# The product for u in one float32 pass, and a shorter read-back of the chunk kernel

## The chip, the cores and the metric

The kernel runs on one core of a Trainium2 chip. The metric is the device time of one execution in microseconds (us), the median of three runs. The engines of a core work in parallel, each through its own queue and in order: PE (TensorE: matrix products and transposes, results in PSUM), DVE (VectorE), ACT (ScalarE), POOL (GpSimd) and SP, which here only issues DMAs. ACT and POOL issue DMAs as well. All DMAs share 16 DMA engines.

## The reference, cut to what matters

One decoder layer on 256 tokens of width 2048, in float32:

```python
h = rmsnorm(x, ln1_g)
q, k, v, u = split(h @ w_in)                  # 1024, 256, 256, 1024 columns
a = sliding_window_attention(q, k, v)         # QK-norm, bias, sinks
y = gelu(S5(u) + d * u)                       # 64 groups of 16 channels, 64 complex states each
s = y * sigmoid(y @ w_glu)
x = x + concat(rmsnorm(a), rmsnorm(s)) @ w_out
x = x + (silu(h2 @ w_gate) * (h2 @ w_up)) @ w_down      # h2 = rmsnorm(x)
```

S5 is a linear recurrence over time with a complex diagonal, one input matrix b and one output matrix c for each group.

## The kernel before

**Large products.** Each large product takes weights in pieces of 256 rows by 512 columns (512 KB), which SP loads into four buffers (`raw`, tag "w"). A piece is split into two parts of a shorter float type, fp32r: `whi`, a copy by ACT (line 455), and `wlo`, the rest by DVE (line 456), two buffers of each. The left operand is split likewise (`hT`, `lT` for x). `block` (lines 490 to 506) adds three products for each of the two 128-token halves: hi x hi, hi x lo and lo x hi, each with 512 columns. A piece so has 12 matmuls. There are 16 pieces for u, 24 for q, k and v, 8 for the GLU, 32 for the output projection and 264 for the SwiGLU.

**x.** Four tiles `xt[0..3]` of 512 KB hold x transposed. They lie in memory that is used later for other things: `sm[0]`, `sm[1]`, `qn[0]`, `qn[1]`. `split_x` writes hT (ACT, 16 instructions) and lT (DVE, 16) with the norm's gain; ACT then squares xt in place for the token sums, from which r1, the norm's factor, comes. The result of the u blocks is scaled by r1 into `qn`, and goes through DRAM (`ud`) to turn it from tokens into chunks.

**The S5 part** works in chunks of T = 8 tokens, in four quarters q of 16 groups, with these steps for each quarter: `matrices` in two halves (m0a, m0b, ...: six DVE operations of 1024 columns each, small PE products and transposes), `tokens` (u0: reads u from DRAM as chunks, transposes it on PE), `rotations` (r0: the angles), `states` (s0: PE products, a scan on DVE), `outputs` (o0: 32 PE products with the chunk's kernel `m` and with the carried state, written to DRAM as `zd`). The string STEPS gives the order in which they are put to the scheduler. `issue_after(marks[n])` holds instructions behind piece n of the weights on the same engine: U_AT for the copy in `tokens` (ACT), PY_AT for `outputs` (PE), GELU_AT for the GELU (ACT). Pieces 0 to 15 are those of u, 16 to 39 those of q, k and v. The blocks of q, k and v run beside the S5 steps; the GLU needs all four quarters.

**The chunk's kernel.** Output t of a chunk takes input s <= t with tap t - s, so `m` is a Toeplitz matrix, [8 inputs x 16 channels, 8 outputs x 16 groups x 16 channels]. `matrices` writes the 8 taps to DRAM (`kd`, four DMAs of 32 KB), behind 7 taps of zeros that were written at the start, and one DMA of 1 MB reads them back with a step of one tap for each input, zeros included. All these DMAs are issued by POOL:

```python
m = self.sp.tile([P, T, GC, GP], F32, name="mt", tag="mt", bufs=2)
nc.gpsimd.dma_start(m.rearrange("p t g q -> p (t g q)"),
                    dap(kd, [[GC * GP, T], [TAPS * GC * GP, GP], [1, T * GC * GP]]))
```

POOL also issues the loads of u's chunks (`ut`), of the S5 result (`sm` from `zd`), and computes the small powers.

Of the kernel before, what the change touches and what calls it, by code (L numbers as in the profile page):

```python
# [2 lines left out]

# [1 line left out]

# [5 lines left out]
F32 = mybir.dt.float32  # L11
# [7 lines left out]
P = 128  # L19
# [20 lines left out]
WORK = dict(tag="t", bufs=4)  # L40


STEPS = "m0a m0b u0 u1 r0 m1a s0 m1b u2 r1 o0 s1 m2a u3 r2 m2b r3 o1 s2 m3a m3b o2 s3 o3"

U_AT = (11, 12, 19, 20)
PY_AT = (21, 27, 34, 39)
GELU_AT = (38, 39, 39, 39)

HEADS = [0, 4, 1, 5, 2, 6, 3, 7, 8, 12, 9, 13, 10, 14, 11, 15]

# [3 lines left out]
C2 = float(np.float32(round((TWO_PI - C1) * 2.0**20) / 2.0**20))  # L54
C3 = float(np.float32(TWO_PI - C1 - C2))
MAGIC = 12582912.0
TAPS = 2 * T - 1
UB = 4 * GP


# [4 lines left out]
def bc(ap, pos, n):  # L65
    dims = [list(d) for d in ap.ap]
    dims.insert(pos, [0, n])
    return bass.AP(ap.tensor, ap.offset, dims)
# [10 lines left out]
class Ssm:  # L79
# [8 lines left out]
    def load(self):  # L88
        self.a = self.sp.tile([P, 2 * G], F32, name="sa")
        self.ldt = self.sp.tile([G, 3], F32, name="ldt")  # L90
        self.nc.sync.dma_start(self.ldt[:, 0:1], self.ins["ssm_log_dt"].rearrange("(g o) -> g o", o=1))
        self.nc.sync.dma_start(self.a, self.ins["ssm_a"])
        self.kts = [self.sp.tile([P, T, 4, GP], F32, name=f"kt{i}") for i in range(2)]
        self.kd = [self.dpool.tile([GP, TAPS, GC * GP], F32, name=f"kd{q}") for q in range(G // GC)]
        zero = self.sp.tile([GP, GC * GP], F32, name="zero")
        self.nc.gpsimd.memset(zero, 0.0)
        for kd in self.kd:
            self.nc.gpsimd.dma_start(kd[:, : T - 1], bc(zero, 1, T - 1))
        self.bc = []
        self.cm, self.bm, self.m, self.u, self.h, self.rot = ([[] for _ in range(G // GC)] for _ in range(6))  # L100
        self.sign = self.sp.tile([P, 1], F32, name="sign")
        self.nc.vector.memset(self.sign, 1.0)
        self.nc.vector.memset(self.sign[NS:], -1.0)
# [127 lines left out]
    def matrices(self, q, h):  # L231

        nc, v, s = self.nc, self.nc.vector, self.nc.scalar
        b, c = self.bc[q]
        ft, lam = self.ft, self.lam
        HG = GC // 2
        hs = slice(h * HG, (h + 1) * HG)
        gh = slice(q * GC + h * HG, q * GC + (h + 1) * HG)
        cmh = self.sp.tile([P, HG, T + 1, GP], F32, name="cm", tag="cm", bufs=4)
        s.activation(cmh[:, :, 0], c[:, 0, hs], AF.Copy, scale=self.sign[:, 0:1])  # L240
        tm = self.sp.tile([P, HG, T, GP], F32, name="tm", tag="tm")
        for dst, i in ((cmh[:, :, 1:], 0), (tm, 1)):
            e = lam[:, i, 1 : T + 1, gh].rearrange("p t g -> p g t")
            v.tensor_tensor(dst, bc(c[:, i, hs], 2, T), bc(e, 3, GP), op=ALU.mult)
        v.tensor_tensor(cmh[:, :, 1:], cmh[:, :, 1:], tm, op=ALU.subtract)
        bmh = self.sp.tile([P, HG, P], F32, name="bm", tag="bm", bufs=4)
        bm2 = self.sp.tile([P, HG, T, GP], F32, name="bm2", tag="bm2", bufs=2)
        tm2 = self.sp.tile([P, HG, T, GP], F32, name="tm2", tag="tm")
        for dst, i in ((bm2, 0), (tm2, 1)):
            e = ft[:, i, :, gh].rearrange("p t g -> p g t")  # L250
            v.tensor_tensor(dst, bc(b[:, i, hs], 2, T), bc(e, 3, GP), op=ALU.mult)
        v.tensor_tensor(bm2, bm2, tm2, op=ALU.add)
        pk = self.ps.tile([P, 2, T, GP], F32, name="pk", **WORK)
        for i in range(HG):
            gq, g4 = divmod(i, 4)
            nc.tensor.matmul(pk[32 * g4 : 32 * g4 + 32, gq].rearrange("p t q -> p (t q)"),
                             lhsT=bm2[:, i, 0:2].rearrange("p t q -> p (t q)"),
                             rhs=cmh[:, i, :T].rearrange("p t q -> p (t q)"), start=True, stop=True)
        kt = self.kts[q % 2]
        kv = kt[:, :, 2 * h : 2 * h + 2]  # L260
        s.copy(kv.rearrange("p t g q -> p g t q"), pk)
        v.tensor_tensor(kv[:, 0], kv[:, 0], self.dg[:, 4 * q + 2 * h : 4 * q + 2 * h + 2], op=ALU.add)
        for n in range(HG // 4):
            pt = self.ps.tile([P, 4, P], F32, name="pt_bm", **WORK)
            for i in range(4):
                nc.tensor.transpose(pt[:, i], bm2[:, 4 * n + i].rearrange("p t q -> p (t q)"), self.cst["ident"])  # L266
            s.copy(bmh[:, 4 * n : 4 * n + 4], pt)
        self.cm[q] += [cmh[:, i, 1:].rearrange("p t q -> p (t q)") for i in range(HG)]
        self.bm[q] += [bmh[:, i] for i in range(HG)]
        if h == 0:  # L270
            return
        kd = self.kd[q]
        for g4 in range(4):
            nc.gpsimd.dma_start(kd[:, T - 1 :, 4 * GP * g4 : 4 * GP * (g4 + 1)],
                                kt[32 * g4 : 32 * g4 + GP].rearrange("p t g q -> p t (g q)"))
        m = self.sp.tile([P, T, GC, GP], F32, name="mt", tag="mt", bufs=2)
        nc.gpsimd.dma_start(m.rearrange("p t g q -> p (t g q)"),
                            dap(kd, [[GC * GP, T], [TAPS * GC * GP, GP], [1, T * GC * GP]]))
        self.m[q] = [m[:, :, 4 * (g % 4) + g // 4] for g in range(GC)]

    def tokens(self, q, behind):

        nc, s = self.nc, self.nc.scalar
        ut = self.sp.tile([P, T, 4 * GP], F32, name="ut", tag="ut")
        nc.gpsimd.dma_start(ut.rearrange("p t x -> p (t x)"),
                            dap(self.ud, [[T * UB, P], [1, T * UB]], 4 * q * L * UB))
        pu = self.ps.tile([P, 4, P], F32, name="pu", **WORK)
        uq = self.sp.tile([P, 4, T, GP], F32, name="uq", tag="uq")
        last = ut[:, T - 1]
        with self.tc.issue_after(behind):  # L290
            s.copy(uq, bass.AP(last.tensor, last.offset, [list(last.ap[0]), [GP, 4], [-UB, T], [1, GP]]))
        for gq in range(4):
            nc.tensor.transpose(pu[:, gq], uq[:, gq].rearrange("p t q -> p (t q)"), self.cst["ident"])
        u = self.sp.tile([P, GC, NCH], F32, name="ua", tag="ua", bufs=4)
        s.copy(u.rearrange("p (a b) c -> p b a c", b=4), pu.rearrange("p b (a c) -> p b a c", c=NCH))
        self.u[q] = u
# [131 lines left out]
class Weights:  # L428
# [8 lines left out]
    def fetch(self, src):  # L437
        w = self.raw.tile([P, KD, NB], F32, name="w", tag="w")
        self.nc.sync.dma_start(w, src)
        self.ready.append(w)  # L440

    def piece(self, src):
        was, self.tc.cur_priority = self.tc.cur_priority, self.place
        out = self._piece(src)
        self.place, self.tc.cur_priority = self.tc.cur_priority, was
        return out
# [14 lines left out]
def layer_kernel(ctx: ExitStack, tc: tile.TileContext, ins, out):  # L461
# [28 lines left out]
    def block(hi, lo, wsrc, k0=0):  # L490
# [14 lines left out]
            wts.marks[-1].append(mm.ins)  # L505
        return acc

    def pieces(w, nb, kg0, kgs):
        return [w[nb, kg] for kg in range(kg0, kg0 + kgs)]

# [51 lines left out]
        ssm.coefficients(0, nc.sync)  # L562
    with prio(-99_990):
        ssm.coefficients(1, nc.sync)
    def split_x(k4):
        for i in range(4):
            k = 4 * k4 + i
            s.activation(hT[:, k], xt[k4][:, i], AF.Copy, scale=g1[:, k : k + 1])
            v.scalar_tensor_tensor(lT[:, k], xt[k4][:, i], g1[:, k : k + 1], hT[:, k].bitcast(F32),
                                   op0=ALU.mult, op1=ALU.subtract)  # L570

    with prio(9_000):
        for k4 in range(4):
            split_x(k4)
    with prio(9_500):
        ssm.tables()
    with prio(9_400):
        for k4 in range(4):
            s.activation(xt[k4], xt[k4], AF.Square)
        ssx = token_sums([xt[k // 4][:, k % 4] for k in range(16)], "ssx", sp, "an")  # L580
        r1 = rsqrt_mean(ssx, D, NT, "r1")


# [13 lines left out]


    ngc = G // GC
    with prio(26_500):  # L600
        for q in range(2, ngc):
            ssm.coefficients(q, nc.sync, sm[q - 2])
    for nb in range(SW // NB):
        with prio(30_000 + 2_000 * nb):
            acc = block(hT, lT, pieces(ins["w_u"], nb, 0, 16 // KD))
            for t in range(NT):
                un = qn[t][:, nb * NB : (nb + 1) * NB]
                s.activation(un, acc[t], AF.Copy, scale=r1[:, t : t + 1])
                nc.scalar.dma_start(ssm.ud[nb * (NB // UB) : (nb + 1) * (NB // UB), t * P : (t + 1) * P]
                                    .rearrange("b p x -> p b x"), un.rearrange("p (b x) -> p b x", x=UB))  # L610
    with prio(60_000):
        for nb in (2, 0, 1):
            acc = block(hT, lT, pieces(ins["w_qkv"], nb, 0, 16 // KD))
# [6 lines left out]
    with prio(20_000):  # L620
        for step in STEPS.split():
# [1 line left out]
            if step[0] == "m":  # L623
                ssm.matrices(q, "ab".index(step[2]))
            elif step[0] == "u":
                ssm.tokens(q, marks[U_AT[q]][0])
            elif step[0] == "r":
                ssm.rot[q] = ssm.rotations(q)
            elif step[0] == "s":
# [275 lines left out]
```

## Time and profile before

| | us |
|---|---|
| median of three runs | 1096.76 (1092.87 to 1099.7) |
| profiled execution, its own time | 1101.14 |
| its span | 1099.3 |
| PE busy in it | 1048.4 (95%) |
| DVE busy | 622.4 (57%) |
| ACT busy | 502.7 (46%) |
| from the start to the first product of the GLU | 201.9 |

The first 204 us hold u, q, k, v and the S5 part; then come the GLU and the attention with the output projection as filler (to about 350 us), and the SwiGLU to the end. From 250 us on PE is busy in nearly every slice.

### The profile page before, as it was taken

To read this page: it belongs to the slowest core of one execution; us is meant where nothing else is said; L and a number is where in the kernel's file an instruction comes from. 1 tells how busy PE (TensorE), PEld (TensorE's weight loads), DVE (VectorE), ACT (ScalarE), POOL (GpSimd) and SP (SyncE) were. 2 spreads that over 40 slices of the span, in tenths; PEclk is the share of its full clock that TensorE was granted. 3 is DMA by queue.
4 is the path that set the end of the run, shared out by engine and by line. 5 is a ranking of instruction groups with operands and counts; after the bars stand their busy time and mean duration, and the time that the engine had idled before them with its cause. 6 is when DMAs were issued, how large, how long until landed. Compare 5 with 4: busy or idle time off the path is not lost.

```text
span 1099.3 us, 13352 instructions
## 1 busy us (share of the span) xinstructions
PE 1048.4 (95%) x5120; PEld 833.5 (76%) x5120; DVE 622.4 (57%) x761; ACT 502.7 (46%) x689; POOL 42.3 (4%) x62
## 2 busy tenths in 40 slices
PE   6999794799999999999999999999999999999998
PEld 4776573577788888888888888888888888888886
DVE  6998685488756544554445544554445444444443
ACT  7454354376546544444444444444444333333332
POOL 1011012500000000000000000000000000000000
PEclk9999898899999999999999999999999999999999
DMA  8766565462455555555555555555555556565653
GB/s 323 222 192 162 131 171 164 146 206 97 135 173 191 168 179 190 190 192 181 187 189 191 191 181 185 191 190 188 186 186 189 190 187 202 189 207 191 209 182 107
DMA packets 62127, 201.45 MB, mean 183 GB/s; under 512 B 11440, under 2 KB 13792, under 8 KB 61296
## 3 DMA queue, kind: packets, MB, share of 16 engines
q1 hardware_dynamic: 52656, 184.83, 51.5%
q0 software_dynamic: 3520, 11.58, 4.1%
q10 hardware_dynamic: 5888, 4.20, 1.3%
q8 instruction: 40, 0.66, 0.3%
q14 instruction: 23, 0.19, 0.1%
HBM read 195.38 MB, written 5.20 MB: 182 GB/s over the span
## 4 chain that ended last, share of the span: by engine, by line
PE 83%; DMA 6%; DVE 6%; ACT 3%; issue 2%; POOL 0%; SPq 0%; ACTq 0%; DVEq 0%; POOLq 0%
PE acc L502 26%; PE acc L503 26%; PE acc L501 26%; DMA w<-in_w_qkv 3%; DVE wlo L456 2%; DMA zd<-za 2%; PE pt_f L833 1%; DMA mt<-kd 1%; ACT whi L455 1%; PE po L745 1%; DMA sa<-in_ssm_a 1%; PE pl L707 0%; PE pp L739 0%; PE pt_bm L266 0%; PE pq L517 0%
## 5 line engine op out<-in xcount | busy, mean ns | idle before, releaser
L456 DVE TENSOR_TENSOR wlo<-w,whi 128x1024 fp32r<-128x1024 f32 x344 | 421.1, 1225 | 411.1 <-ACT whi L455 410.8
L455 ACT CAST whi<-w 128x1024 fp32r<-128x1024 f32 x344 | 362.1, 1053 | 495.5 <-PE acc L503 474.3
L502 PE MATMUL acc<-wlo,pTh 128*128 128x512 f32 x704 | 276.3, 392 | 0.1
L503 PE MATMUL acc<-whi,pTl 128*128 128x512 f32 x704 | 276.0, 392 | 0.1
L501 PE MATMUL acc<-whi,pTh 128*128 128x512 f32 x704 | 274.5, 390 | 0.0
L503 PEld LDWEIGHTS acc<-whi,pTl 128*128 128x128 f32 x704 | 133.3, 190 | 26.6 <-DVE pTl L537 0.5
L501 PEld LDWEIGHTS acc<-whi,pTh 128*128 128x128 f32 x704 | 132.2, 188 | 27.6 <-ACT pTh L536 0.5
L502 PEld LDWEIGHTS acc<-wlo,pTh 128*128 128x128 f32 x704 | 132.2, 188 | 27.4 <-DVE wlo L456 0.5
L502 PE MATMUL acc<-wlo,fhi 128*128 128x512 f32 x352 | 140.5, 399 | 0.0
L501 PE MATMUL acc<-whi,fhi 128*128 128x512 f32 x352 | 138.7, 394 | 0.0
L503 PE MATMUL acc<-whi,flo 128*128 128x512 f32 x352 | 138.1, 392 | 0.0
L502 PE MATMUL acc<-wlo,hT 128*128 128x512 f32 x160 | 65.9, 412 | 13.9 <-DVE wlo L456 13.8
L501 PEld LDWEIGHTS acc<-whi,fhi 128*128 128x128 f32 x352 | 66.1, 188 | 17.2
L503 PEld LDWEIGHTS acc<-whi,flo 128*128 128x128 f32 x352 | 66.1, 188 | 15.6
L502 PEld LDWEIGHTS acc<-wlo,fhi 128*128 128x128 f32 x352 | 66.1, 188 | 15.2
L501 PE MATMUL acc<-whi,hT 128*128 128x512 f32 x160 | 62.8, 407 | 12.0 <-ACT whi L455 12.0
L503 PE MATMUL acc<-whi,lT 128*128 128x512 f32 x160 | 65.3, 408 | 0.0
L501 PE MATMUL acc<-whi,mT 128*128 128x512 f32 x128 | 50.9, 398 | 0.8 <-ACT mT L536 0.8
L502 PE MATMUL acc<-wlo,mT 128*128 128x512 f32 x128 | 50.5, 394 | 0.0
L503 PE MATMUL acc<-whi,nT 128*128 128x512 f32 x128 | 50.3, 394 | 0.0
L502 PEld LDWEIGHTS acc<-wlo,hT 128*128 128x128 f32 x160 | 30.9, 193 | 24.7 <-DVE wlo L456 17.7
L501 PEld LDWEIGHTS acc<-whi,hT 128*128 128x128 f32 x160 | 30.8, 194 | 20.2 <-ACT whi L455 13.2
(251 smaller groups left out, 771.0 us busy)
## 6 DMA issues: line engine op xcount, KB each, us to landing
w<-in_w_gu SPq DMA_DIRECT2D x176, 512.0 KB, 3.5
w<-in_w_down SPq DMA_DIRECT2D x88, 512.0 KB, 4.3
w<-in_w_out SPq DMA_DIRECT2D x32, 512.0 KB, 3.5
w<-in_w_qkv SPq DMA_DIRECT2D x24, 512.0 KB, 3.8
w<-in_w_u SPq DMA_DIRECT2D x16, 512.0 KB, 4.5
mt<-kd POOLq DMA_DIRECT2D x4, 1024.0 KB, 15.4
w<-in_w_glu SPq DMA_DIRECT2D x8, 512.0 KB, 4.9
bias<-td POOLq DMA_DIRECT2D x4, 512.0 KB, 4.5
```

The source lines that it names most:

```text
L455: self.marks.append([nc.scalar.copy(hi, w).ins])
L456: nc.vector.tensor_tensor(lo, w, hi.bitcast(F32), op=ALU.subtract)
L501: mm = pe.matmul(acc[t], lhsT=xh, rhs=whi, start=first, stop=False)
L502: pe.matmul(acc[t], lhsT=xh, rhs=wlo, start=False, stop=False)
L503: pe.matmul(acc[t], lhsT=xl, rhs=whi, start=False, stop=last)
L745: pe.matmul(po[a * HD : (a + 1) * HD, :, t], lhsT=kvn[kb][:, kv * HD : (kv + 1) * HD], rhs=pT[:, b, a], start=kb == 0, stop=kb == t)
L833: pe.transpose(pt[:, i, t * P : (t + 1) * P], act[t][:, i * P : (i + 1) * P], ident)
```

## The change

The products for u use x and the weights as they are, in float32 (`block32`, `whole`): one matmul in place of three, no split of the 16 pieces. x is scaled in place by DVE (`scale_x`); the squares go to tiles of their own before that; `split_x` is done later, by four copies of ACT and four subtractions of DVE over 1024 columns, and only for q, k and v. u's result goes to two buffers `un` instead of qn. A first ACT instruction loads its table at the start.

The zero taps in DRAM are gone. `mt` becomes two standing tiles, set to zero once by POOL, and eight DMAs for each quarter read only the taps 0 to t for input T - 1 - t, 16 partitions each, 16 to 128 KB. The order of the steps and the marks are new; u0 and u1 have no mark, the outputs stand behind pieces 14, 19, 25 and 32 (before 21, 27, 34 and 39).

```diff
-STEPS = "m0a m0b u0 u1 r0 m1a s0 m1b u2 r1 o0 s1 m2a u3 r2 m2b r3 o1 s2 m3a m3b o2 s3 o3"
+STEPS = "m0a m0b r0 u0 m1a u1 s0 m1b r1 o0 u2 m2a s1 u3 m2b r2 o1 m3a s2 m3b r3 o2 s3 o3"
-U_AT = (11, 12, 19, 20)
-PY_AT = (21, 27, 34, 39)
-GELU_AT = (38, 39, 39, 39)
+U_AT = (0, 0, 18, 19)
+PY_AT = (14, 19, 25, 32)
+GELU_AT = (34, 35, 36, 37)
...
-        self.kd = [self.dpool.tile([GP, TAPS, GC * GP], F32, name=f"kd{q}") for q in range(G // GC)]
-        zero = self.sp.tile([GP, GC * GP], F32, name="zero")
-        self.nc.gpsimd.memset(zero, 0.0)
-        for kd in self.kd:
-            self.nc.gpsimd.dma_start(kd[:, : T - 1], bc(zero, 1, T - 1))
+        self.kd = [self.dpool.tile([GP, T, GC * GP], F32, name=f"kd{q}") for q in range(G // GC)]
+        self.mts = [self.sp.tile([P, T, GC, GP], F32, name=f"mt{i}") for i in range(2)]
+        for m in self.mts:
+            self.nc.gpsimd.memset(m, 0.0)
...
-        m = self.sp.tile([P, T, GC, GP], F32, name="mt", tag="mt", bufs=2)
-        nc.gpsimd.dma_start(m.rearrange("p t g q -> p (t g q)"),
-                            dap(kd, [[GC * GP, T], [TAPS * GC * GP, GP], [1, T * GC * GP]]))
+        m = self.mts[q % 2]
+        for t in range(T):
+            nc.gpsimd.dma_start(m[GP * t : GP * (t + 1), T - 1 - t :].rearrange("p t g q -> p t (g q)"), kd[:, : t + 1])
...
+    def whole(self, src):
+
+        was, self.tc.cur_priority = self.tc.cur_priority, self.place
+        if not self.ready:
+            self.fetch(src)
+        w = self.ready.pop(0)
+        self.place, self.tc.cur_priority = self.tc.cur_priority, was
+        self.marks.append([None])
+        return [w[:, i] for i in range(KD)]
...
+    def block32(x, wsrc):
+
+        acc = [ps.tile([P, NB], F32, name=f"acc{t}", tag="mm") for t in range(NT)]
+        nk = KD * len(wsrc)
+        k = 0
+        for src in wsrc:
+            for w in wts.whole(src):
+                for t in range(NT):
+                    mm = pe.matmul(acc[t], lhsT=x(k)[:, t * P : (t + 1) * P], rhs=w, start=k == 0, stop=k == nk - 1)
+                k += 1
+            wts.marks[-1].append(mm.ins)
+        return acc
...
-    def split_x(k4):
+    with prio(-310_000):
+        warm = cpool.tile([P, 1], F32, name="warm")
+        v.memset(warm, 1.0)
+        s.activation(warm, warm, AF.Square)
+    sq = [sp.tile([P, 4, L], F32, name=f"sq{k4}", tag="bm", bufs=4) for k4 in range(4)]
+
+    def scale_x(k4):
         for i in range(4):
             k = 4 * k4 + i
-            s.activation(hT[:, k], xt[k4][:, i], AF.Copy, scale=g1[:, k : k + 1])
-            v.scalar_tensor_tensor(lT[:, k], xt[k4][:, i], g1[:, k : k + 1], hT[:, k].bitcast(F32),
-                                   op0=ALU.mult, op1=ALU.subtract)
+            v.tensor_scalar_mul(xt[k4][:, i], xt[k4][:, i], g1[:, k : k + 1])
+
+    def split_x(k4):
+        ks = slice(4 * k4, 4 * k4 + 4)
+        s.copy(hT[:, ks], xt[k4])
+        v.tensor_tensor(lT[:, ks], xt[k4], hT[:, ks].bitcast(F32), op=ALU.subtract)
...
-    with prio(26_500):
-        for q in range(2, ngc):
-            ssm.coefficients(q, nc.sync, sm[q - 2])
     for nb in range(SW // NB):
         with prio(30_000 + 2_000 * nb):
-            acc = block(hT, lT, pieces(ins["w_u"], nb, 0, 16 // KD))
+            acc = block32(lambda k: xt[k // 4][:, k % 4], pieces(ins["w_u"], nb, 0, 16 // KD))
             for t in range(NT):
-                un = qn[t][:, nb * NB : (nb + 1) * NB]
+                un = sp.tile([P, NB], F32, name="un", tag="hh", bufs=2)
...
+    with prio(20_100):
+        for k4 in range(4):
+            split_x(k4)
+        for q in range(2, ngc):
+            ssm.coefficients(q, nc.sync, sm[q - 2])
...
-                ssm.tokens(q, marks[U_AT[q]][0])
+                ssm.tokens(q, q > 1 and marks[U_AT[q]][0])
```

## Rows read from the trace of the kernel before

**Rows 1.** Windows: length, PE, PEld, DVE, ACT, POOL busy, PEclk, DMA share, GB/s.

```profile
10.00:76.00 66.00, 63.00 (x325) 48.73 (x325) 63.04 (x121) 41.59 (x64) 5.07 (x9) 1.00 0.80 252
76.00:106.00 30.00, 27.33 (x258) 20.02 (x257) 26.33 (x32) 13.90 (x23) 3.31 (x6) 0.94 0.70 172
106.00:150.00 44.00, 35.76 (x271) 28.36 (x271) 34.16 (x41) 23.53 (x39) 4.01 (x7) 0.92 0.50 138
150.00:182.00 32.00, 26.96 (x235) 19.80 (x233) 22.30 (x28) 16.47 (x28) 5.78 (x10) 1.00 0.66 174
182.00:204.00 22.00, 8.11 (x83) 5.49 (x84) 5.66 (x10) 4.17 (x9) 1.51 (x3) 0.69 0.35 96
204.00:250.00 46.00, 41.23 (x189) 29.45 (x188) 35.07 (x67) 28.08 (x58) 16.24 (x15) 1.00 0.64 206
```

**Rows 2.** Waits of PE, 0 to 205 us: total, times, longest.

```profile
PE acc L502 <- DVE wlo L456: 13.8, 7, 8.0
...
PE py L349 <- DMA mt<-kd: 9.4, 1, 9.4
PE pg L333 <- DVE gg L331: 4.3, 1, 4.3
...
PE acc L501 <- ACT zT L657: 0.9, 1, 0.9
PE acc L503 <- DVE wT L658: 0.7, 1, 0.7
```

**Rows 3.** Chain that ended last: start, us, what, its longest DMA pieces.

```profile
78.66 15.18 DMA w<-in_w_qkv
...
107.09 13.95 DMA zd<-za
...
150.59 14.07 DMA w<-in_w_qkv
...
182.29 13.04 DMA mt<-kd
```

**Rows 4.** DMA issues: count, KB each, median us to landing.

```profile
w<-in_w_qkv SPq DMA_DIRECT2D x24, 512.0 KB, 3.8
...
mt<-kd POOLq DMA_DIRECT2D x4, 1024.0 KB, 15.4
...
zd<-za ACTq DMA_DIRECT2D x4, 256.0 KB, 2.6
...
kd<-kt POOLq DMA_DIRECT2D x16, 32.0 KB, 2.9
```

**Rows 5.** Windows, 188 to 194 us.

```profile
188.00:194.00 6.00, 0.00 (x0) 0.00 (x0) 0.06 (x1) 0.00 (x0) 0.00 (x0) 0.50 0.50 113
```

**Rows 6.** Timeline of PE inside the u product: first and last of 15 matmuls.

```profile
44.70 0.39 PE L501 MATMUL acc<-whi,hT 128*128 128x512 f32 x1
...
47.88 0.39 PE L503 MATMUL acc<-whi,lT 128*128 128x512 f32 x1
```

**Rows 7.** Chain: float32 products of 512 columns: one, then two.

```profile
97.52 2.05 PE pg L333 x2
...
253.40 1.72 PE pl L707 x4
```

**Rows 8.** Groups of DVE, 0 to 60 us: count, busy us, mean ns.

```profile
L456 DVE TENSOR_TENSOR wlo<-w,whi 128x1024 fp32r<-128x1024 f32 x16 | 19.4, 1219 | 1.8 <-ACT whi L455 1.8
```

**Rows 9.** Timeline of the start: ACT and PE.

```profile
8.05 1.04 ACT L455 CAST whi<-w 128x1024 fp32r<-128x1024 f32 x1 [0.54 <-DMA w<-in_w_u]
...
9.15 1.22 PE L501 MATMUL acc<-whi,hT 128*128 128x512 f32 x2 [9.15 <-ACT whi L455]
```

**Rows 10.** Timeline of POOL: its work on the kernel's read-back, a memset.

```profile
175.88 2.12 POOL L274 DMA_DIRECT2D kd<-kt  x4 [3.43 <-DVE kt L262]
...
182.29 0.64 POOL L277 DMA_DIRECT2D mt<-kd  x1
...
204.92 0.97 POOL L664 MEMSET kT<- 128x1024 f32 x1
```

More of the change, by code (lines that the diff above doesn't have):

```diff
@@ L1 @@
 import math
-from contextlib import ExitStack, contextmanager
+from contextlib import ExitStack, contextmanager, nullcontext
 import numpy as np
@@ L56 @@
 MAGIC = 12582912.0
-TAPS = 2 * T - 1
 UB = 4 * GP
@@ L273, in matrices @@
         for g4 in range(4):
-            nc.gpsimd.dma_start(kd[:, T - 1 :, 4 * GP * g4 : 4 * GP * (g4 + 1)],
+            nc.gpsimd.dma_start(kd[:, :, 4 * GP * g4 : 4 * GP * (g4 + 1)],
                                 kt[32 * g4 : 32 * g4 + GP].rearrange("p t g q -> p t (g q)"))
-        m = self.sp.tile([P, T, GC, GP], F32, name="mt", tag="mt", bufs=2)
-        nc.gpsimd.dma_start(m.rearrange("p t g q -> p (t g q)"),
-                            dap(kd, [[GC * GP, T], [TAPS * GC * GP, GP], [1, T * GC * GP]]))
+        m = self.mts[q % 2]
+        for t in range(T):
+            nc.gpsimd.dma_start(m[GP * t : GP * (t + 1), T - 1 - t :].rearrange("p t g q -> p t (g q)"), kd[:, : t + 1])
         self.m[q] = [m[:, :, 4 * (g % 4) + g // 4] for g in range(GC)]
@@ L289, in tokens @@
         last = ut[:, T - 1]
-        with self.tc.issue_after(behind):
+        with self.tc.issue_after(behind) if behind else nullcontext():
             s.copy(uq, bass.AP(last.tensor, last.offset, [list(last.ap[0]), [GP, 4], [-UB, T], [1, GP]]))
@@ L564, in layer_kernel @@
         ssm.coefficients(1, nc.sync)
-    def split_x(k4):
+    with prio(-310_000):
[4 more added lines that the diff above has]
+    def scale_x(k4):
         for i in range(4):
             k = 4 * k4 + i
-            s.activation(hT[:, k], xt[k4][:, i], AF.Copy, scale=g1[:, k : k + 1])
-            v.scalar_tensor_tensor(lT[:, k], xt[k4][:, i], g1[:, k : k + 1], hT[:, k].bitcast(F32),
-                                   op0=ALU.mult, op1=ALU.subtract)
+            v.tensor_scalar_mul(xt[k4][:, i], xt[k4][:, i], g1[:, k : k + 1])
[3 more added lines that the diff above has]
+        v.tensor_tensor(lT[:, ks], xt[k4], hT[:, ks].bitcast(F32), op=ALU.subtract)
     with prio(9_000):
         for k4 in range(4):
-            split_x(k4)
+            if k4 == 0:
+                for i in range(4):
+                    s.activation(sq[0][:, i], xt[0][:, i], AF.Square)
+            else:
+                s.activation(sq[k4], xt[k4], AF.Square)
+            scale_x(k4)
     with prio(9_500):
@@ L577, in layer_kernel @@
     with prio(9_400):
-        for k4 in range(4):
-            s.activation(xt[k4], xt[k4], AF.Square)
-        ssx = token_sums([xt[k // 4][:, k % 4] for k in range(16)], "ssx", sp, "an")
+        ssx = token_sums([sq[k // 4][:, k % 4] for k in range(16)], "ssx", sp, "an")
         r1 = rsqrt_mean(ssx, D, NT, "r1")
```

## The prediction

> **What bounds the kernel now.** I read the page's share of busy time first: PE is busy for 1048 of 1099 us, so a gain has to come from the 51 us in which it isn't, or from PE work that goes away. Next come the windows, to find where those 51 us lie [rows 1]. After 250 us there is next to nothing. The subject is the first 204 us, and in them two stretches differ. From 10 to 76 us, where most of the u product lies, PE misses 3.0 us of 66, though DVE is full (63.04). From 76 to 204 us, PE misses 2.7, 8.2, 5.0 and 13.9 us in the four stretches, 29.8 us together. The granted clock also falls there, to means of 0.94, 0.92 and 0.69: in an idle spell it goes to 0.50, 1.2 of 2.4 GHz [rows 5], and PE comes back at that. If all of that lies on busy time, it costs 30 x 0.06 + 44 x 0.08 + 8.1 x 0.31 = 7.8 us; I take 7. So some 37 us between 76 and 204 us could be had.
>
> The four stretches are cut so that each holds one read-back of the chunk's kernel (`mt<-kd`, 1 MB). The chain of waits shows what it does [rows 3]: beside the first and the third, a weight piece takes 15.18 and 14.07 us; beside the second, the store of the S5 result takes 13.95; the fourth is itself on the chain with 13.04. The DMA issues give the usual time of these transfers: 3.8 us for a piece, 2.6 for the store, 15.4 for the read-back [rows 4]. The slow store is the worst of it, as the next quarter's `zz` needs the buffer that it empties: DVE waits in order before `zz`, the weight splits queue behind it, and PE waits up to 8.0 us for `wlo` [rows 2]. In the fourth stretch PE waits 9.4 us for the read-back itself [rows 2]. While that read-back is alone in flight, the DMA engines' mean share is 0.50 at 113 GB/s [rows 5]: as if half of the engines carried it, and a transfer that needs all of them waits for those.
>
> **Part 1, the float32 product.** Before: 16 pieces x 12 = 192 matmuls. From the first to the last of 15 in a row it is 47.88 - 44.70 = 3.18 us over 14 steps, 0.227 us each [rows 6], so 43.6 us. After: 16 x 4 = 64 matmuls. No large float32 product is in the trace of before; the nearest rows have the same 512 columns and a 128 x 128 left operand, and each product is written as two instructions. Two products of the attention logits in a row take 1.72 us, 0.86 each; a lone one, in a stretch whose mean clock is 0.94, takes 2.05 [rows 1, 7]. I take 0.86, since the u product is a dense row of them: 64 x 0.86 = 55.0 us. PE gets **+11.4 us** of work on the path. The dearer row is the upper end; nothing speaks for less than 0.86.
>
> **Part 2, the start.** The first matmul waits for ACT's split of the first piece: the copy begins as the piece lands at 8.05 and the matmul begins at 9.15 [rows 9]. Now PE takes the piece as it lies; x's first chunk must be there by then too, and needs one short scaling. **-1.1 us.** The two memsets of `mt` on POOL have 2048 columns each; one of 1024 takes 0.97 us [rows 10], so 3.9 us, in place of four DMA issues and a small memset. I cost them at nothing: POOL has 5.07 us of work between 10 and 76 us [rows 1]. Uncovered, they would put the S5 tables off by 3.9 us at most, not PE.
>
> **Part 3, DVE and ACT.** 16 splits of 1.22 us leave DVE (19.4 us, [rows 8]) and as many copies leave ACT. The split of x shrinks from 16 instructions on each engine to 4, of the size of a weight split (4 x 1.22 = 4.9 us on DVE), and 16 scalings come. While PE takes its 55 us for u, DVE has no weight split to do and can do the S5 matrices. That takes away the waits on `wlo` and `whi` inside the u product: of the 3.0 us missed up to 76 us I take **-2**. The moved split of x costs nothing as long as it is done before u ends (8.1 + 55.0 us, and what PE does for S5 in between); if not, PE waits for one copy and one subtraction, some 2.3 us. The loads of b and c for quarters 2 and 3 go into the memory of x's first half. Their four issues now stand on SP behind the last read of it, with weight pieces queued behind them. Four buffers at 4 x 0.86 = 3.4 us a piece cover 10 us; I cost this at nothing. `un` shares two buffers with `hh`, which the outputs of quarter 0 free; ACT waits there, and PE only if that lasts a whole block, as PSUM holds the results of two.
>
> **Part 4, the read-back.** 36 of 64 taps are read, so 0.59 MB of 1.05. At the rate of before that is 15.4 x 36/64 = 8.7 us. From below, eight issues of 0.53 us (2.12 / 4, [rows 10]) and 2.9 us to land [rows 4] make 7.1. I take 8.7. POOL issues 12 DMAs for a quarter in place of 5, some 3.7 us more, ahead of the loads of `ut` and `sm`; that is small beside the 30 us and more that lie between two quarters [rows 3]. The eight wait for the outputs two quarters earlier, which read the same tile, as before. A stop of 8.7 us in the weight stream is covered by four raw buffers of 12 x 0.227 = 2.7 us each, 10.9 us; one of 15.4 was not. With the stops go the slow store and DVE's wait behind it.
>
> The Trainium skill, in "DMA: Bandwidth & Descriptors", section "Why a DMA increments its semaphore by 16 and not by 1", says that a copy runs on the largest number of engines, up to 16, that divides the slowest dimension of both sides. By that the old read-back with its outermost 8 has 8 engines, which the share of 0.50 agrees with, and the new ones with 16 have all; the transfers would then take some 2.6 us, an estimate, beside the issues' 4.2.
>
> **Part 5, the order.** The outputs of the last quarter stand behind piece 32 instead of 39, and the GELUs behind 34 to 37. Before, the last outputs and the GLU's first product had no piece left to cover them, hence the 13.9 us. Now seven pieces (19 us) lie behind them, against a tail of a store (2.6 us, [rows 4]), a load of the same size, the GELU and a transpose. DVE has what it needs: between 76 and 204 us it was busy 88 of 128. What I leave standing of the 37 us: the wait of `pg` for the scan, 4.3, the two waits at the GLU's start, 0.9 + 0.7 [rows 2], and half of the clock loss, 3.5; 9.4 together. So **-27.4**. From 204 to 250 us PE misses 4.8 us while DVE, ACT and POOL prepare the attention [rows 1]; k and v can now be prepared ahead of the GLU, for which I take **-1**.
>
> **The sum.** +11.4 - 1.1 - 2 - 27.4 - 1 = -20.1 us, against the profiled execution: 1101.1 to 1081. That execution lies 4.4 us above the median of the runs, so against the median, 1096.8 to **1077**. If nothing is left standing, it is 1067.
>
> **The rivals.** (a) DVE and the S5 chain become the bound: the matrices of quarter 2 need buffers that the outputs of quarter 0 free, and those stand behind piece 14, late in a u product that is now longer; quarter 3 then comes after piece 32 and half of the 37 us stays. For it: DVE is full up to 76 us. Against: 19.4 us of it are the splits that go. -18.5 in place of -27.4 gives 1086.
>
> (b) The float32 product costs more than its row: PE meets x and the weights as they come from DMA, and where it waits for them its clock falls. If a quarter of the 64 products cost the 2.05 us of the lone one, that is 16 x 1.19 = 19 us more: 1096. Against: from 10 to 76 us the clock was granted in full at 252 GB/s [rows 1], and the float32 product asks for 0.5 MB in 3.4 us, 150 GB/s.
>
> (c) The slower one: the eight small reads run one after the other. A 32 KB DMA takes 2.9 us to land [rows 4]; eight in series are 23.2 us, 7.8 more than before, and the outputs stand earlier in PE's queue, so PE stops at them. If the wait of 9.4 us grows to 17.2 and comes at two quarters, the 34 us eat what the order gave: +11.4 - 3 - 37 + 34 + 4 of half clock = +9, 1106. It decides once the waits before `py` pass 27 us in total. Against: the four writes of 32 KB are issued 0.53 us apart and overlap. The Trainium skill, same page, section "Rules for kernel authors", speaks for this rival: it asks to join small transfers, as under 64 KB one pays mostly overhead. No row here shows eight reads of this kind.
>
> (d) More than forecast: all waits go, and the attention's start overlaps better (3 us): 1064.
>
> **How the numbers follow.** Forecast (1070 to 1085): 0.58. (a): 0.17, (b): 0.08, (c): 0.09, (d): 0.08. The range leaves out (b)'s upper part and (c): 1062 to 1096. One per cent, 11 us, is about what a measurement of this kernel can tell from no change. Faster by more than that (below 1086) are the forecast, (d) and a third of (a): 0.72. Within it: most of (a) and (b), 0.18. Slower: (c) and a little more, 0.10.
>
> **What would show it.** The u product's matmuls come in steps of 0.43 us, first at about 8.1 us, and u ends between 70 and 85 us. DVE has no full stretch there. Each read-back lands within 10 us, no piece beside it takes above 10, the store keeps to 3. The first GLU product comes at 176 to 188 us in place of 201.9, and the sum of PE's missing time between 76 us and there is below 12. From 250 us on nothing changes. The prediction is wrong if PE waits at `py` or for `whi` at the change from u to q, k and v by more than a few us, or if the steps are above 0.5 us.

## The result and the profile after

The changed kernel takes 1078.57 us (median of 4 runs, 1076.3 to 1080.04), the kernel before beside it 1095.35 (1092.87 to 1099.7): a ratio of 0.986 [0.983, 0.989]. The profiled executions are 1101.14 us before and 1079.72 after, with spans of 1099.3 and 1077.9.

The page's share of busy time, after:

```profile
PE 1055.7 (98%) x5056; PEld 822.3 (76%) x5056; DVE 608.3 (56%) x750; ACT 485.2 (45%) x665; POOL 56.5 (5%) x87
```

PE is busy for 7 us more than before, in a span that is 21.4 us shorter. The windows show where the idle time went; the first six answer to [rows 1], the last is a cut of the second:

```profile
10.00:76.00 66.00, 65.48 (x284) 31.22 (x283) 55.64 (x116) 22.72 (x40) 8.40 (x16) 1.00 0.68 211
76.00:106.00 30.00, 26.02 (x205) 18.59 (x207) 20.19 (x26) 13.77 (x22) 7.92 (x15) 0.94 0.65 180
106.00:150.00 44.00, 43.37 (x428) 33.33 (x421) 40.79 (x50) 24.82 (x41) 10.70 (x19) 1.00 0.55 162
150.00:182.00 32.00, 29.69 (x194) 23.65 (x193) 18.48 (x23) 18.39 (x29) 9.53 (x16) 1.00 0.69 196
182.00:204.00 22.00, 20.52 (x79) 15.28 (x78) 13.99 (x27) 10.77 (x15) 10.20 (x8) 0.84 0.72 246
204.00:250.00 46.00, 44.81 (x213) 32.33 (x214) 39.23 (x78) 35.76 (x93) 2.38 (x2) 1.00 0.41 137
80.00:90.00 10.00, 6.09 (x34) 3.47 (x33) 5.44 (x7) 2.36 (x3) 0.59 (x1) 0.84 0.53 154
```

The time that PE misses falls from 3.0 to 0.5 us between 10 and 76 us, from 29.8 to 8.4 between 76 and 204, and from 4.8 to 1.2 between 204 and 250. Of the 8.4, 3.9 lie between 80 and 90 us. The waits of PE up to 205 us answer to [rows 2]:

```profile
PE acc L524 <- DMA w<-in_w_u: 7.8, 1, 7.8
PE pg L331 <- DVE gg L329: 4.5, 3, 3.9
PE pt_z L691 <- ACT sm L689: 3.7, 2, 2.2
PE pu L291 <- ACT uq L289: 0.5, 1, 0.5
```

The waits for `wlo` (8.0 us at worst) and for the read-back before `py` (9.4) are gone. The chain that ended last, the lines that answer to [rows 3, 7]:

```profile
1.66 6.00 DMA w<-in_w_u
...
20.31 21.66 PE acc L524 x50
...
43.67 4.53 DMA ud<-un
...
48.85 2.96 DMA ut<-ud
...
178.66 4.56 DMA sm<-zd
```

No weight piece after the first, no store of the S5 result and no read-back of the kernel is on it up to 204 us. And the DMA issues, against [rows 4]:

```profile
w<-in_w_qkv SPq DMA_DIRECT2D x24, 512.0 KB, 4.1
...
ud<-un ACTq DMA_DIRECT2D x4, 256.0 KB, 5.6
...
zd<-za ACTq DMA_DIRECT2D x4, 256.0 KB, 3.4
...
kd<-kt POOLq DMA_DIRECT2D x16, 32.0 KB, 2.4
mt<-kd POOLq DMA_DIRECT2D x4, 128.0 KB, 6.1
...
mt<-kd POOLq DMA_DIRECT2D x4, 32.0 KB, 2.3
```

The largest strip of the read-back lands in 6.1 us where the 1 MB took 15.4. POOL's timeline has its eight issues, first to last in 3.85 us:

```profile
57.52 3.85 POOL L276 DMA_DIRECT2D mt<-kd  x8 [2.04 <-DMA kd<-kt]
```

So, by the medians, a read-back is over some 10 us after its first issue.

### The profile page after: what moved, and what is told of

Its sections match the earlier page's. It is cut to its first block, busy times and chain, and to the rows that moved or that the text cites. A ratio compares the mean times of both kernels' runs of the same rounds, so it can differ in the third digit from the quotient of the medians.

```text
span 1077.9 us, 13217 instructions
## 1 busy us (share of the span) xinstructions
PE 1055.7 (98%) x5056; PEld 822.3 (76%) x5056; DVE 608.3 (56%) x750; ACT 485.2 (45%) x665; POOL 56.5 (5%) x87
## 4 chain that ended last, share of the span: by engine, by line
PE 94%; DVE 2%; DMA 2%; ACT 1%; issue 1%; SPq 0%; ACTq 0%; POOLq 0%
PE acc L510 27%; PE acc L511 27%; PE acc L509 27%; PE acc L524 5%; PE pt_f L868 1%; ACT whi L463 1%; DVE wlo L464 1%; PE pt_bm L264 1%; PE pl L742 1%; DMA w<-in_w_u 1%; PE po L780 1%; PE pg L331 0%; PE pp L774 0%; DMA sm<-zd 0%; DMA ud<-un 0%
## 5 line engine op out<-in xcount | busy, mean ns | idle before, releaser
L464 DVE TENSOR_TENSOR wlo<-w,whi 128x1024 fp32r<-128x1024 f32 x328 | 401.8, 1225 | 417.9 <-ACT whi L463 417.5
L463 ACT CAST whi<-w 128x1024 fp32r<-128x1024 f32 x328 | 344.2, 1049 | 481.7 <-PE acc L511 465.9
L510 PEld LDWEIGHTS acc<-wlo,fhi 128*128 128x128 f32 x352 | 66.3, 188 | 15.4
L524 PE MATMUL acc<-w,sm 128*128 128x512 f32 x64 | 30.8, 629 | 7.8 <-DMA w<-in_w_u 7.8
L509 PE MATMUL acc<-whi,hT 128*128 128x512 f32 x96 | 38.3, 404 | 0.0
L510 PE MATMUL acc<-wlo,hT 128*128 128x512 f32 x96 | 38.1, 396 | 0.1
L511 PE MATMUL acc<-whi,lT 128*128 128x512 f32 x96 | 38.0, 396 | 0.0
L861 ACT ACTIVATE sl<-acc,r 128x256 f32<-128x256 f32 x44 | 20.8, 472 | 20.8 <-PE acc L511 20.8
```

Source lines behind the costliest of these rows:

```text
L463: self.marks.append([nc.scalar.copy(hi, w).ins])
L464: nc.vector.tensor_tensor(lo, w, hi.bitcast(F32), op=ALU.subtract)
L509: mm = pe.matmul(acc[t], lhsT=xh, rhs=whi, start=first, stop=False)
L510: pe.matmul(acc[t], lhsT=xh, rhs=wlo, start=False, stop=False)
L511: pe.matmul(acc[t], lhsT=xl, rhs=whi, start=False, stop=last)
L524: mm = pe.matmul(acc[t], lhsT=x(k)[:, t * P : (t + 1) * P], rhs=w, start=k == 0, stop=k == nk - 1)
```

## The experiments

My theory after the result: the read-back's shape is the whole gain, through the transfers that it held up; the float32 product is a cost that this gain pays. The rivals: the gain needs the new order, or the time that DVE and ACT no longer spend on splits; or it comes from the bytes that are no longer read.

**The read-back alone** (`readback_alone`): before, with the change's `kd`, standing tiles and eight reads. The product for u stays split, the order stays the old one.

```diff
-        m = self.sp.tile([P, T, GC, GP], F32, name="mt", tag="mt", bufs=2)
-        nc.gpsimd.dma_start(m..., dap(kd, [[GC * GP, T], [TAPS * GC * GP, GP], [1, T * GC * GP]]))
+        m = self.mts[q % 2]
+        for t in range(T):
+            nc.gpsimd.dma_start(m[GP * t : GP * (t + 1), T - 1 - t :]..., kd[:, : t + 1])
```

> The kernel before with the new read-back alone (standing tiles, eight DMAs of the nonzero taps, no zeros in DRAM); u product, order and marks as before. Theory (the 1 MB read-back causes the stops of the weight stream, the store and the outputs): no weight piece beside a read-back takes above 8 us, the S5 store takes 2 to 4 us, PE misses at most 15 of the 29.8 us between 76 us and the GLU, and as no float32 cost comes in, the time is 1070 to 1080. Rival (the gain is DVE's relief and the order): the waits stay in other places, 1090 to 1096.

Measured: 1076.61 us (1075.55 to 1077.43), 0.982 [0.975, 0.988] of the kernel before; that can't be told from the change itself. Its windows and its DMA issues:

```profile
76.00:106.00 30.00, 29.32 (x280) 22.95 (x279) 29.87 (x38) 17.38 (x30) 11.77 (x23) 1.00 0.69 190
106.00:150.00 44.00, 43.44 (x324) 33.60 (x324) 43.60 (x53) 26.23 (x40) 7.54 (x14) 1.00 0.63 179
150.00:182.00 32.00, 22.04 (x247) 17.34 (x246) 15.86 (x22) 14.14 (x27) 11.62 (x20) 0.84 0.43 126
182.00:204.00 22.00, 19.88 (x88) 14.28 (x88) 14.87 (x29) 12.21 (x20) 11.87 (x9) 1.00 0.81 264
```

```profile
w<-in_w_qkv SPq DMA_DIRECT2D x24, 512.0 KB, 3.7
...
zd<-za ACTq DMA_DIRECT2D x4, 256.0 KB, 2.1
...
mt<-kd POOLq DMA_DIRECT2D x4, 128.0 KB, 5.7
```

The stretches 76 to 150 and 182 to 204 us run nearly full, with the outputs still behind pieces 21 to 39. Only 150 to 182 stays idle for 10 us. The pieces of q, k and v are used up by 162 us there, and PE then stands twice before the first product of the GLU at 177.67, for the last quarter's scan and for its read-back:

```profile
166.44 1.30 PE L332 MATMUL pg<-gg,pack 128*128 128x512 f32 x2 [4.57 <-DVE gg L330]
...
171.85 0.65 PE L348 MATMUL py<-mt,ua 128*32 128x128 f32 x8 [4.11 <-DMA mt<-kd]
```

This is the stop that lay between 182 and 204 us before (4.3 and 9.4 us, [rows 2]), shorter and some 20 us earlier.

**The change without its read-back** (`old_readback`): after, with the zero taps, the tag `mt` and the one 1 MB read of before.

```diff
-        m = self.mts[q % 2]
-        for t in range(T):
-            nc.gpsimd.dma_start(m[GP * t : GP * (t + 1), T - 1 - t :]..., kd[:, : t + 1])
+        m = self.sp.tile([P, T, GC, GP], F32, name="mt", tag="mt", bufs=2)
+        nc.gpsimd.dma_start(m..., dap(kd, [[GC * GP, T], [TAPS * GC * GP, GP], [1, T * GC * GP]]))
```

> The changed kernel with the old read-back (zero taps in DRAM, one DMA of 1 MB). Theory: the stops come back, weight pieces beside the read-back take 11 us and more, and the time is 1092 to 1102, the cost of the float32 product with little gain. Rival (order and DVE's relief make the gain): 1079 to 1084.

Measured: 1109.37 us (1108.28 to 1111.39), 1.012 [1.005, 1.019]: slower than before, and above the 1092 to 1102 that I had written. The chain again has the three stalls of [rows 3]:

```profile
63.24 12.99 DMA w<-in_w_qkv
...
109.69 15.39 DMA zd<-za
...
173.08 15.97 DMA mt<-kd
```

So the rest of the change (the float32 product with its `un` tiles, and the order) loses time with the old read-back; the new one takes some 31 us away from it.

**The change with the old order** (`old_order`): after, with the old `STEPS` and marks (u0 and u1 still have none).

```diff
-U_AT = (0, 0, 18, 19)
-PY_AT = (14, 19, 25, 32)
-GELU_AT = (34, 35, 36, 37)
+U_AT = (11, 12, 19, 20)
+PY_AT = (21, 27, 34, 39)
+GELU_AT = (38, 39, 39, 39)
```

> The changed kernel with the order of steps and the marks of before (u0 and u1 without a mark, as their piece now has no ACT copy to stand behind). Theory: the last outputs and all GELUs stand behind the last piece again, so PE misses 8 to 13 us ahead of the GLU: 1087 to 1092. Rival (with a fast read-back the order matters little): 1077 to 1082.

Measured: 1080.69 us (1079.3 to 1081.68), 0.986 [0.979, 0.992]. That is 2.1 us above the change, no difference by the intervals. My theory (1087 to 1092) failed and its rival held: in the change, the order is worth little beside the new read-back.

**The change with the split product** (`split_u`): `readback_alone` with the new order on top; u is computed with split x and weights as before.

The edit against `readback_alone`, with `STEPS` as in the change and no mark for u0 and u1:

```diff
-U_AT = (11, 12, 19, 20)
-PY_AT = (21, 27, 34, 39)
-GELU_AT = (38, 39, 39, 39)
+U_AT = (0, 0, 18, 19)
+PY_AT = (14, 19, 25, 32)
+GELU_AT = (34, 35, 36, 37)
```

> The kernel before with the new read-back and the new order and marks, but the u product split in three as before. Theory (PE is the bound once the stops are gone, so the float32 product is a cost of 11.4 us): 1066 to 1072, below the changed kernel. Rival (the float32 product pays for itself, since without the splits DVE is free for the S5 steps): DVE is full to 76 us and late after it, 1079 to 1088.

Measured: 1072.75 us (1072.43 to 1073.22), 0.978 [0.971, 0.986], 5.8 us below the change. Against the change it puts back three split matmuls for one float32, and with them the old split of x and u's result in `qn`. So the float32 product and what came with it cost, but less than the product's 11.8 us of work. Against `readback_alone` it is 3.9 us less, and each of its four runs lies below each of the four there. The stop before the GLU is shorter:

```profile
166.44 1.10 PE L332 MATMUL pg<-gg,pack 128*128 128x512 f32 x2 [1.98 <-DVE gg L330]
168.80 0.66 PE L348 MATMUL py<-mt,ua 128*32 128x128 f32 x8 [1.27 <-DMA mt<-kd]
```

So with the split product the order is worth some 4 us.

**The bytes or the shape** (`strips_full`, `two_halves`). Both read 1 MB with the zeros, as before. The first takes it in eight strips of 16 partitions, the second in two DMAs of the old form, whose outermost dimension is 4 at the source.

```diff
-        nc.gpsimd.dma_start(m..., dap(kd, [[GC * GP, T], [TAPS * GC * GP, GP], [1, T * GC * GP]]))
+        for t in range(T):                                   # strips_full
+            nc.gpsimd.dma_start(m[GP * t : GP * (t + 1)]..., kd[:, t : t + T])
...
+        for i in range(2):                                   # two_halves
+            nc.gpsimd.dma_start(m[64 * i : 64 * (i + 1)]..., dap(kd, [[GC * GP, T // 2], ...], i * ...))
```

> The kernel before, with one edit: the 1 MB read-back, zeros included, is issued as eight DMAs of 16 partitions and 128 KB each, whose outermost dimension is 16 on both sides (before: 8 at the source). Same bytes, same order. Theory (the old form runs on half of the DMA engines, and that is what stops the others): the eight land within 8 us of their issue, weight pieces beside them within 8 us, and the time is within 4 us of the read-back of nonzero taps alone: 1075 to 1081. Rival (the bytes count, the zeros among them): the last lands after 13 us and more, and the time is 1086 to 1094.

> The kernel before, with one edit: the 1 MB read-back is issued as two DMAs of 64 partitions, whose outermost dimension at the source is 4 each. Theory (the outermost dimension sets how many engines carry a copy): 128 KB for each engine as before or worse, so each lands after 14 us and more, and the time is 1088 to 1100, no gain. Rival (one big DMA is slow, several smaller ones are fast whatever their shape): they land within 9 us, 1076 to 1083.

Measured: strips 1087.79 us (1086.84 to 1088.68, 10 runs), 0.993 [0.990, 0.996]; halves 1093.88 (1089.97 to 1100.67, 10 runs), 1.001 [0.997, 1.004]. The read-back among the DMA issues, of the strips:

```profile
mt<-kd POOLq DMA_DIRECT2D x32, 128.0 KB, 5.3
```

and of the halves, with three pieces of their chain:

```profile
mt<-kd POOLq DMA_DIRECT2D x8, 512.0 KB, 15.6
```

```profile
78.72 13.48 DMA w<-in_w_qkv
107.27 14.60 DMA w<-in_w_qkv
142.97 13.62 DMA w<-in_w_qkv
```

On the transfer the answer is plain. The same megabyte lands in 5.3 us a strip, some 9 us from first issue to last landing, when each read has 16 partitions outermost; halving the size of a DMA, with 4 outermost in place of 8, does nothing, and weight pieces beside it still take 13 to 15 us. Nor is it a matter of 1 MB from POOL's queue: the reads of x's rows for the residual, in the before and the after kernel alike, have that size and that queue, with 128 outermost:

```profile
x<-in_x POOLq DMA_DIRECT2D x2, 1024.0 KB, 6.8
```

The Trainium skill's rule on the slowest dimensions ("DMA: Bandwidth & Descriptors", "Why a DMA increments its semaphore by 16 and not by 1") says which of the two should help, and these rows agree with it.

On the time my expectation for the strips failed: 1087.8 where 1075 to 1081 was written. The weight-piece stalls are gone there, but the compiled program is another one. In PE's order, 335 weight matmuls stand ahead of quarter 0's first `py`, against 295 before and 285 in `readback_alone`, and PE reaches that `py` at 107.8 us, against 102.4 and 94.9. POOL's timeline shows a possible cause:

```profile
98.89 2.39 POOL L274 DMA_DIRECT2D kd<-kt  x4 [18.43 <-DVE kt L262]
...
113.50 0.76 POOL L651 DMA_DIRECT2D sm<-zd  x1 [11.64 <-DVE cm L245]
114.25 3.87 POOL L278 DMA_DIRECT2D mt<-kd  x8
```

`kd` was written by some 103 us, but the read-back is issued at 114.25, behind a load of `sm` that waits for the outputs.

**Standing tiles or order** (`strips_standing`, `strips_ordered`, `one_ordered`). The first gives the strips standing tiles in place of a tag. The second keeps the tag and makes each load of `sm` from `zd` follow the next quarter's read-back. The third does the same to the kernel before, with its one read.

```diff
+        m = self.mts[q % 2]                                  # strips_standing
...
+        self.read.append(d.ins)                              # the other two
...
+                with tc.issue_after(ssm.read[min(q + 1, ngc - 1)]):
+                    nc.gpsimd.dma_start(sm[t]..., ssm.zd...)
```

> The kernel before with the 1 MB read-back in eight strips, zeros included, as in the earlier run of strips, but into standing tiles. Theory (in the earlier run the transfers were fast, and the gain was lost since POOL issued the second and third read-back 10 us and more after their writes had landed, behind a load that waits for the S5 store): if the standing tiles put the read-back ahead of that load again, 1075 to 1080; if POOL's order stays as it was, 1085 to 1090, and the bytes then count no more than the order. Rival (1 MB costs more than 0.59 MB on the way): read-backs early and yet 1083 and more.

> The kernel before with the 1 MB read-back in eight strips, and the load of each S5 quarter's result put behind the next quarter's read-back on POOL. Theory (fast strips in time are all that the change's gain needs; the zeros cost little): each read-back is issued within 6 us of its writes, and the time is 1075 to 1081. Rival (the fewer bytes of the nonzero taps matter as well): read-backs early, yet 1084 to 1090.

> The kernel before with its single 1 MB read-back, and only the order on POOL changed as in the run beside it. Theory (the order is a second condition, the shape the first): the read-back takes 13 to 17 us still and stops weight pieces and stores, 1088 to 1098. Rival (the order on POOL alone makes the gain): 1075 to 1083.

Measured: 1087.5 us (1086.62 to 1089.31, 5 runs), 0.992 [0.990, 0.995]; 1097.94 (1095.19 to 1099.22, 10 runs), 1.002 [1.000, 1.005]; 1094.68 (1091.88 to 1104.09, 10 runs), 1.001 [0.997, 1.004]. Standing tiles give nothing; the read-back still comes behind that load. The forced order does issue the strips early (102.91 us), and is slower than the strips by 10 us, which neither my theory nor its rival had. Two pieces of its chain, and its largest waits of PE inside the weight stream:

```profile
110.23 8.78 DMA zd<-za
...
151.81 8.01 DMA zd<-za
```

```profile
PE acc L504 <- DVE wlo L458: 13.3, 6, 5.3
```

The store that is issued while the strips are still landing is slow (median 5.5 us, against 2.9 in `strips_full`), and DVE and the splits queue behind it as in the kernel before. Weight pieces are in flight as well, so it isn't shown that the strips alone slow it. PE's order stayed the late one (335 matmuls). With one read the forced order changes nothing.

**Where the float32 product's price lies** (`un_own`, `split_u_warm`, `f32_first`). In the change, the tiles `un` of u's result share two buffers with `hh` of the S5 scan. Four views of the changed kernel, of ACT's queue, DVE and PE, show what comes of it:

```profile
76.98 0.40 ACTq L639 DMA_DIRECT2D ud<-un  x1
...
78.20 0.37 ACTq L639 DMA_DIRECT2D ud<-un  x1
```

```profile
74.74 1.23 DVE L464 TENSOR_TENSOR wlo<-w,whi 128x1024 fp32r<-128x1024 f32 x1 [2.20 <-ACT whi L463]
83.66 0.69 DVE L323 TENSOR_TENSOR hh<-pb,sn 128x512 f32<-128x512 f32 x1 [7.69 <-ACT whi L463]
```

```profile
86.48 1.80 PE L331 MATMUL pg<-gg,pack 128*128 128x512 f32 x2 [3.91 <-DVE gg L329]
```

The second half's stores of `un` leave at 76.98 and 78.20 us and take 6.6 and 6.2 to land, the first so until some 83.6. DVE stands before `hh` until 83.66, the profile's guess at a releaser (`whi`) having been done long before (in `old_order`, with the same buffers, the profile names the store of `un` itself, for 8.0 us); the weight splits queue behind it, PE stops for 3.9 us, and the granted clock between 80 and 90 us is 0.84. `un_own` gives `un` its own two buffers:

```diff
-                un = sp.tile([P, NB], F32, name="un", tag="hh", bufs=2)
+                un = sp.tile([P, NB], F32, name="un", tag="un", bufs=2)
```

> The changed kernel with two buffers of its own for u's result un, in place of the two that it shares with hh of the states. Theory (in the changed kernel the store of un takes 5.6 us, hh waits for it, and DVE stands from 76 to 83.7 us with the weight splits behind, so PE misses 3.9 us and goes to half clock): the stop goes, 1072 to 1075, within 3 us of the kernel with the split product. Rival (DVE stood there for the weight pieces, which come late): 1077 to 1080.

Measured: 1074.46 us (1073.5 to 1075.42), 0.980 [0.977, 0.984], 4.1 us below the change (0.986 [0.983, 0.989]; the intervals just touch). So most of the 5.8 us between the change and `split_u` comes from these buffers; the 1.7 us that are left can't be told from nothing, and where the product's added PE work is won back no run shows. DVE in `un_own` goes on where the change's stands, and the whole stretch is granted 0.99:

```profile
76.84 1.23 DVE L464 TENSOR_TENSOR wlo<-w,whi 128x1024 fp32r<-128x1024 f32 x1 [2.30 <-ACT whi L463]
79.16 2.36 DVE L242 TENSOR_TENSOR cm<-sm,lam 128x1024 f32<-128x1024 f32 x2 [1.09 <-PE py L351]
```

```profile
76.00:204.00 128.00, 120.37 (x900) 92.54 (x899) 91.88 (x118) 69.65 (x107) 36.08 (x53) 0.99 0.65 202
```

`split_u_warm` is `split_u` with the change's first ACT instruction, which loads the activation table before x arrives:

```diff
+    with prio(-310_000):
+        warm = cpool.tile([P, 1], F32, name="warm")
+        v.memset(warm, 1.0)
+        s.activation(warm, warm, AF.Square)
```

> The kernel with the split product, the new read-back and the new order, and the early table load of ACT as well, as a candidate for the fastest. Theory: the first matmul waits for the weight piece and ACT's copy of it, which the table load doesn't stand before, so nothing changes beyond 1 us: 1072 to 1074. Rival (the load of 1.28 us before the first split of x is on the path of the start): 1070 to 1072.

Measured: 1071.10 us (1070.44 to 1072.31), 0.979 [0.975, 0.983], the lowest median of all. By the ratios it can't be told from `split_u` (0.978) or `un_own` (0.980).

`f32_first` takes only the first half of u in float32 and the second split, with x split ahead of u:

```diff
-            acc = block32(lambda k: xt[k // 4][:, k % 4], pieces(ins["w_u"], nb, 0, 16 // KD))
+            if nb == 0:
+                acc = block32(lambda k: xt[k // 4][:, k % 4], pieces(ins["w_u"], nb, 0, 16 // KD))
+            else:
+                acc = block(hT, lT, pieces(ins["w_u"], nb, 0, 16 // KD))
```

> The changed kernel, but only the first half of u's columns is taken in float32; the second is split in three, with the split of x ahead of it. Theory (the float32 product is a cost of PE time): half of the 5.8 us by which the changed kernel lies above the one with the split product comes back, 1074 to 1077. Rival (the cost lies in one place, at the start or at the step from u to q, k and v): either nothing comes back, 1078 to 1080, or all, 1071 to 1073.

Measured: 1080.44 us (1079.77 to 1082.5), 0.987 [0.983, 0.992]: above all the ranges that I had written, and inconclusive. The GLU starts earlier than in any other version (172.0 us, against 181.8 in the change), but the attention's start gives it back. Its waits of PE up to 250 us:

```profile
PE pp L778 <- DVE lg L770: 4.7, 1, 4.7
PE pt_k L723 <- DVE kvn L719: 3.5, 1, 3.5
```

## Why the prediction was right

The forecast was 1077 us, the measurement 1078.57; the profiled execution was forecast at 1081 and took 1079.72. The terms, one by one:

**Part 1**, +11.4: right. The chain has 50 float32 instructions in 21.66 us, 0.433 each, two to a product: 0.866 us, and 64 of them 55.4. Rival (b) is out. **Part 2**, -1.1: PE's first matmul starts at 7.79 us in place of 9.15, -1.4; the memsets of `mt` (3.55 us) lie on an idle POOL. **Part 3**, -2: PE misses 0.5 us of 66 in place of 3.0, -2.5. But `un` in the buffers of `hh`, which I costed at nothing, cost 4 us. I had asked only whether ACT waits for the outputs of a quarter to free them; the wait runs the other way, `hh` standing behind a store of `un`.

**Part 4**: 8.7 us were forecast for a read-back, and it takes about 10 (3.85 of issues, 6.1 for the last strip). The estimate of 2.6 us for the transfers on all engines was too low. Rival (c) is out: the strips overlap, and PE waits nowhere at `py`. The rule of the Trainium skill that it leaned on ("DMA: Bandwidth & Descriptors", "Rules for kernel authors"), to join small transfers, doesn't decide here: eight reads of 16 to 128 KB beat one of 1 MB.

**Part 5**, -27.4: the size is nearly right, the reason only in part. From 76 to 204 us PE misses 8.4 us, and the clock costs 30 x 0.06 + 20.5 x 0.16 = 5.1: 13.5 in place of the 9.4 that I left standing, so -23.3. `un` is the difference: without its stop, in `un_own`, the same sum is 7.6 + 18.5 x 0.08 = 9.1. But I put the last 13.9 us down to the order alone, to the seven pieces that now lie behind the outputs. The stop there was 4.3 + 9.4 us [rows 2]; with the new read-back in the old order (`readback_alone`) it is 4.6 + 4.1, and with the new order too (`split_u`) 2.0 + 1.3. So the read-back took some 5 us of the stop and the order as much again. In the change neither wait is left ahead of the GLU, and with the old order (`old_order`) there is none either, at a cost of 2.1 us that can't be told from nothing; that the longer u product gives the S5 part time there is likely, and not shown. Rival (a) is out too: DVE is at 55.64 of 66 us in the first stretch. **204 to 250 us**: -3.6 in place of -1.

Together: +11.8 - 1.4 - 2.5 - 23.3 - 3.6 = -19.0 of the span's -21.4; some 2 us I can't place. Two errors, `un` for the worse and the attention's start for the better, nearly cancel in the total, so that it came this close is in part luck. Of the marks named ahead, u ends at 77.1 us (70 to 85), the first product of the GLU starts at 181.8 (176 to 188), and PE misses 6.9 us from 76 to 182 (below 12). The slowest weight piece of q, k and v takes 6.1 us (10). The store of the S5 result doesn't keep to 3: its median is 3.4, its longest 5.0.

What was shown: without the read-back's change the rest is slower than before, and with it alone the whole gain is there. The shape of the read, not a DMA's size, decides how long it takes and whether weight pieces beside it stall. That the shape alone makes the gain, my theory after the result, was not shown: `strips_full` has the shape and all the bytes, and gains 6 us of some 16. What stays open is where the other 11 us between it and `readback_alone` come from. The zeros' bytes and the later place of the outputs in PE's order both differ, and the kernel made to part them (`strips_ordered`) moved the store into the strips' way and left PE's order late.

## What to carry to other kernels

When transfers that are usually short take four times as long, look for one transfer in flight beside them, and at its DMA share: here a read at half share held up the transfers beside it, and its cost stood in their rows. Cut such a read so that 16 partitions are outermost on both sides, even into many small DMAs; leave out bytes that nobody needs, too, as the new shape with all the bytes gained only 6 us here. And when one change does several things, time each alone: here one part gave some 16 us by itself (1092.5 to 1076.6, by medians), and another, which cost 4 to 6 us, was hidden under it.

## What the runs showed of the hardware

One DMA of 1 MB with 8 outermost takes 15.4 us, two of 512 KB with 4 outermost 15.6 each, eight of 128 KB with 16 outermost 5.3 each, from the same memory to the same tiles. Beside the first two, a 512 KB weight piece takes 13 to 15 us, where its median is about 4. Beside quick strips and weight pieces in flight, a 256 KB store took 8.78 and 8.01 us in `strips_ordered`. Eight issues on POOL take 3.9 us, 0.48 each, and in the changed kernel no wait of PE up to 205 us leads to them.
